# The last two value products of the attention moved among the products of the output projection, and the turning of x's maxima put into the transposing mode

## The chip, the cores and the metric

The kernel runs on one core of a Trainium2 chip. The metric is the time of one execution on the device in microseconds (us), the median over several runs. A profile is one more execution, taken with the hardware profiler, with a trace of every instruction on the five engines: TensorE (PE for its matmuls, PEld for its weight loads), VectorE (DVE), ScalarE (ACT), GpSimd (POOL) and SyncE (SP), which here only issues DMAs.

## The reference, cut to what matters

One encoder layer over 1024 tokens of width 1024, all in float32:

```
h = x @ w_in                                   # 1024 x 1024 by 1024 x 3328
q_a, k_a, v_a, z_a, q_b, k_b, v_b, z_b = split(h)
y_a = neighborhood_attention(q_a, k_a, v_a, rel_pos_bias)     # 8 heads of 64, window 8 x 16 on a grid of 16 x 64
y_b = windowed_gqa_with_sink(rotary(q_b), rotary(k_b), v_b)   # 8 query heads, 2 key heads, |i - j| <= 128
mixed = concatenate([y_a * silu(z_a), y_b * silu(z_b)])
y = mixed @ w_out                              # 1024 x 1024 by 1024 x 1024
out = layer_norm(2 ** 0.25 * x + y, gain, bias)
```

## The kernel before, in words

**Numbers in two halves.** Each operand of a large product is scaled by a power of two and split into a float16 high part and a float16 rest. A product is then three matmuls: high by high, high by rest, rest by high. The scales come from maxima. For x, `x_max` gathers maxima of each partition, line 639 reduces them to `gm` (128 partitions by 1), `x_turn` (L514) brings the 128 values into every partition by a matmul of `gm`, broadcast, with the identity, and `x_scale` (L518) reduces these with VectorE and makes `xsc`, the factor for x's float16 parts. `x_turn` writes to spare columns (320 to 448) of a PSUM bank whose first 320 columns hold a running product of x with the value weights (L627, float32r). Two other places turn maxima the same way, but with `nc.tensor.transpose`: L719 for v and L1086 for w_out.

**The order of the work** around x_turn is written out by hand. From there on TensorE's program is made of "fill" work, which is the projections (L404) and later the output projection (L1165), and of attention work that is put between it. A loop over steps `i` (L1328) runs 128 attention units, four to a quad. In it, per unit: scores (`stage_mm`, L933), bias, sum and minimum on VectorE (L958), exponential on ScalarE (L974), split into two float16 parts on ScalarE (L992) and VectorE (L993), and a DMA that transposes the parts (L999, issued by SP, tile `tr`). Per quad: the value product (`stage_pv`, L1035), 24 matmuls that take the transposed probabilities `tr` and the gathered values `va` and write one half of the bank `ps_t`; and `stage_z` (L1046), where VectorE multiplies that half with the gate into tile `z`. The tables `PV_AT` and `Z_AT` (L1321 to L1324) say at which step each quad's value product and gate multiplication are issued; quads 30 and 31 are the last. `LO` (L1153) is the number of steps that the loop runs past the last unit.

**The fill** is dealt out by `pump_to(u)` (L1056): `FILL_AT` holds steps, `FILL_N` the number of matmuls between one such step and the next, and at each call as many matmuls are issued as the tables say are due. What the tables do not cover follows behind the loop, by `pump(10 ** 6)`. The last fill items are the output projection's first parts, for the four row groups of `mixed` that are done early (tiles m4 to m7, `EO[:4]`): two banks `ps_pj` and one `ps_s` for token tiles 0 to 2, then 24 matmuls into two banks `ps_s` for token tiles 3 and 4, then 12 each into two more banks `ps_s` for the second column half of token tiles 0 and 1. Each matmul is 128x128 by 128x512.

**The end**, `final()` (L1182): the tiles m0 to m3 (the groups that the last value products complete) are split by ScalarE (L1076) and VectorE (L1077); w_out's parts wo8 to wo15 are split by ScalarE (L1121, L1123), VectorE (L1129, L1131) and GpSimd (L1191, L1129); TensorE first multiplies token tile 2's second half for m4 to m7 into `ps_t`, the bank that the value products used, then m0 to m3 for the eight open banks, 24 matmuls for each of the four, and then the remaining token tiles. VectorE adds the residual (L1215) as soon as a bank is complete; the row normalisation and the stores follow. Within `final()` a scheduler of the compiler may change the order; inside the loop the order is that of the code.

Of the kernel before, what the change touches and what calls it, by code (L numbers as in the profile page):

```python
# [38 lines left out]
SCALE_AT = ((4, 6), (7, 2))  # L39
K_ORDER = (5, 0, 6, 1, 7, 2, 3, 4)  # L40
FILL = ORDER[NPRO:]
FILL_AT = [0, 6.6, 13.4, 21.4, 29.4, 37.4, 45.4, 53.4, 61.4, 70, 78.8, 87.6, 96.4, 105, 113, 122, 125, 127, 128.5, 131.5, 136]
ZTAG = {"z3": "zv", "zb3": "zc", "z2": "zs", "zb1": "zd", "zb2": "ze"}
X2POOL = (1, 3, 5)
WVPOOL = (3, 5)
# [29 lines left out]
def hybrid_block(ctx, tc, xT, x, wt, wv, wo, bias, sink, gain, lbias, cos, sin, bmask, out):  # L75
# [305 lines left out]
    def project(name):  # L381
        n = ORDER.index(name)
        w_split(2 * n + 2)
        for half in range(2):
            ps = new_group()
            for k in range(KT):
                if k % 4 == 0:
                    need(w_ops[2 * n + k // 4])
                h, l = parts[2 * n + k // 4]
                if n + 2 < NPRO and half == 0 and k == 4:  # L390
                    w_scan(2 * n + 4)
                if n + 2 < NPRO and half == 1 and k == 0:
                    w_scan(2 * n + 5)
                if half == 0 and k == 4:
                    w_split(2 * n + 3)
                if n + 2 < NPRO and half == 1 and k == 3:
                    z_tree(n + 2)
                if n + 2 < NPRO and half == 1 and k == 7:
                    w_scale(n + 2)
                for i, (a, b) in enumerate(((h, x16h), (h, x16l), (l, x16h))):  # L400
                    mv = b[half, k]
                    if name[0] == "q" and name[1] != "b":
                        mv = mv.rearrange("p (r b c) -> p b r c", b=4, r=8)
                    nc.tensor.matmul(ps, a[:, k % 4, :], mv,  # L404
                                     start=(k == 0 and i == 0), stop=(k == KT - 1 and i == 2))
                    if not (k == KT - 1 and i == 2):
                        yield
            groups.append(evac(name, half, ps))
            yield
# [26 lines left out]
    with ExitStack() as vctx:  # L436
# [76 lines left out]

        def x_turn(ps):  # L514
            nc.tensor.matmul(ps[:, 320:448], gm.to_broadcast([128, 128]), identf, start=False, stop=True,
                             skip_group_check=True)

        def x_scale(ps):  # L518
            nc.vector.tensor_reduce(gm, ps[:, 320:448], axis=AXX, op=ALU.max)
# [97 lines left out]
        for k in range(KT):  # L617
            if k + 3 < KT:
                ahead(k + 3)
            if k + 4 == KT:  # L620
                for j in range(KT):
                    nc.sync.dma_start(x1[j], xT[1, j])
                x_max(6, xh[6].bitcast(F32))
            for ps in FIRST if k == 0 else SECOND if k == 1 else ([(t, a, i) for i in range(3)] for t, a in T1):
                for t, a, i in ps:
                    lh, rh = ((xh, wvh), (xl, wvh), (xh, wvl))[i]
                    nc.tensor.matmul(banks[t, a][:, :320], lh[k][:, 128 * t:128 * t + 128],  # L627
                                     rh[k][:, 320 * a:320 * a + 320],
                                     start=(k == 0 and i == 0), stop=(k == KT - 1 and i == 2))
                if k > 1:  # L630
                    g = T1.index((t, a))
                    if (k, g) == SCALE_AT[0]:
                        wv_scale(banks[t, a])
                        for j in range(KT):
                            wv_hi(j)
                        x_max(7, xh[7].bitcast(F32))
                        for j in range(4):
                            x_max(8 + j, x1pair[j])
                        nc.vector.tensor_reduce(gm, xm, axis=AXX, op=ALU.max)
                        wv_lo(0)  # L640
                    if (k, g) == SCALE_AT[1]:
                        x_turn(banks[t, a])
                        x_scale(banks[t, a])
                        nc.vector.tensor_scalar(vo, vo, xrs, 0.5, op0=ALU.mult, op1=ALU.mult)
# [405 lines left out]
        at(WIN_AT[b], window, b)  # L1050
    run_to(48 * NPRO)
    fill.extend(project(n) for n in FILL)
    FILL_N = [48] * len(FILL) + [9, 9, 6, 12, 24]
    pumped = [0]

    def pump_to(u):  # L1056
        n = 0
        k = int(u) % 4
        u = int(u) // 4 * 4 + 4 * (WARP[k] + (WARP[k + 1] - WARP[k]) * (u - int(u)))
        for k, c in enumerate(FILL_N):  # L1060
            u0, u1 = FILL_AT[k], FILL_AT[k + 1]
            n += int(c * min(max((u - u0) / (u1 - u0), 0), 1))
# [87 lines left out]
            m_ops[e].append(enq("pool", lambda h=h: nc.gpsimd.tensor_sub(  # L1150
                ml[e][:, h], zt[e][:, h], mh[e][:, h]), o))

    LO = 10  # L1153
    NU = len(units)
    def out_mms(t, a, ps, es, c=None):
        o, w = (0, 512) if c is None else LAST[c]
# [162 lines left out]
        stage_mm(us)  # L1319

    PV_AT = {4 * q + 11: q for q in range(30)}  # L1321
    PV_AT.update({131: 30, 135: 31})
    Z_AT = {4 * q + 13: q for q in range(30) if q not in (24, 25, 28, 29)}
    Z_AT.update({115: 24, 116: 25, 128: 28, 129: 29, 132: 30, 136: 31})  # L1324

    clock["step"] = 0
    scan_ops = []
    for i in range(-LD, NU + LO):  # L1328
        if 0 <= i + LD < NU:
# [162 lines left out]
```

## Time and profile before

| | us |
|---|---|
| runs | 441.48, 439.92, 439.67 |
| median of the runs | 439.92 |
| the profiled execution, its own time | 441.73 |
| its span, first to last instruction | 439.9 |
| PE busy | 431.2 |
| DVE busy | 347.8 |
| ACT busy | 298.8 |
| POOL busy | 212.7 |

All times of instructions below are from the profiled execution and count from its span's start. In a timeline row the first number is the start, the second the length from the first start to the last end of the merged instructions, `xN` their number, and what stands in brackets is the idle time of the engine ahead of them and what ended it. The recorded lengths of matmuls overlap, since they are pipelined; the time that one costs is the distance from its start to the next start.

### The profile page before, as it was taken

What the parts mean: (1) busy time and instruction counts of PE and PEld (TensorE: products, weight loads), DVE (VectorE), ACT (ScalarE), POOL (GpSimd) and SP (SyncE); (2) the same over time, 40 slices, a digit from 0 to 9 for tenths busy, and PEclk for the clock granted to TensorE, in tenths of its full rate; (3) what the DMA queues carried; (4) which work ended last, traced back from release to release, by engine and by line L of the source; (5) the groups of instructions that cost most, each with busy time, mean ns of one, the idle gap of its engine ahead of it and who ended that gap; (6) DMA issues with size and microseconds to landing.
All of it is one profiled execution on the core that took longest, in us unless ns stands there. A gap on an engine that the chain in (4) does not pass through costs nothing. (4 is left out here: it accounts for less than half of the span.)

```text
span 439.9 us, 8798 instructions
## 1 busy us (share of the span) xinstructions
PE 431.2 (98%) x2955; PEld 233.2 (53%) x2955; DVE 347.8 (79%) x897; ACT 298.8 (68%) x697; POOL 212.7 (48%) x204
## 2 busy tenths in 40 slices
PE   9999999999999999999999999999999989999994
PEld 8987754444444545454545455554545544444442
DVE  5999947929989988988888887887879739089954
ACT  6798359877577988877889899879787756002211
POOL 0305743564845868356333455566652158005840
PEclk9999999999999999999999999999999999999999
DMA  8992088967946978776999899999999979101721
GB/s 296 343 339 71 5 259 250 302 247 254 322 113 136 168 147 171 141 145 143 173 154 201 138 190 223 192 202 217 216 208 225 193 166 363 41 1 72 262 74 72
DMA packets 133981, 81.72 MB, mean 186 GB/s; under 512 B 101296, under 2 KB 113328, under 8 KB 133680
## 3 DMA queue, kind: packets, MB, share of 16 engines
q1 hardware_dynamic: 133504, 80.67, 74.4%
q8 instruction: 23, 0.38, 0.3%
q10 hardware_dynamic: 432, 0.49, 0.3%
q14 instruction: 22, 0.18, 0.1%
HBM read 50.73 MB, written 9.96 MB: 138 GB/s over the span
## 5 line engine op out<-in xcount | busy, mean ns | idle before, releaser
L404 PE MATMUL ps_pj<-xf,wh 128*128 128x512 f16 x672 | 201.2, 379 | 0.0
L404 PE MATMUL ps_pj<-xf,wl 128*128 128x512 f16 x336 | 127.5, 380 | 0.0
L404 PEld LDWEIGHTS <-wh 128*128 128x128 f16 x672 | 64.9, 98 | 75.4 <-issue 0.8
L1165 PEld LDWEIGHTS <-m 128*128 128x128 f16 x408 | 38.7, 98 | 43.7
L974 ACT ACTIVATE ps_s<-sn,nm 128x385 f32<-128x385 f32 (+3 forms) x96 | 52.1, 543 | 13.9 <-DVE nm L958 12.5
L992 ACT ACTIVATE split<-ps_s,ri 128x384 f16<-128x384 f32 (+2 forms) x96 | 48.5, 539 | 18.3 <-ACT ps_s L974 11.7
L993 DVE SCALAR_TENSOR_TENSOR split<-ps_s,ri,split 128x384 f16<-128x384 f32 (+2 forms) x96 | 52.0, 570 | 5.6 <-ACT split L992 4.6
L1165 PE MATMUL ps_s<-wo,m 128*128 128x512 f16 (+1 forms) x240 | 53.3, 374 | 0.0
L404 PEld LDWEIGHTS <-wl 128*128 128x128 f16 x336 | 32.8, 98 | 38.5 <-issue 0.3
L219 POOL TENSOR_SCALAR wr<-wr,wsc 128x512 f32<-128x512 f32 x26 | 22.4, 862 | 46.9 <-ACT wh L214 45.5
L958 DVE CUSTOM_DVE_ANT_0 sn<-ps_s,bm,nsk 128x384 f32<-128x384 f32 (+1 forms) x64 | 39.7, 635 | 6.6 <-PE ps_s L933 6.4
L901 POOL TENSOR_SCALAR bias<-bias,rsg 128x552 f32<-128x552 f32 (+1 forms) x24 | 20.0, 834 | 45.8 <-DMA bias<-in_bias 33.9
L958 DVE CUSTOM_DVE_ANT_0 sn<-ps_s,bias,sg 128x264 f32<-128x264 f32 (+1 forms) x64 | 33.9, 543 | 2.3 <-PE ps_s L933 1.6
L933 PE MATMUL ps_s<-ks,qs 64*128 64x384 f16 (+4 forms) x384 | 33.4, 305 | 0.1
L220 POOL TENSOR_TENSOR wl<-wr,wh 128x512 f16<-128x512 f32 x26 | 31.8, 1223 | 2.2
L1222 ACT ACTIVATE sd<-mv,eps 128x1 f32<-128x1 f32 x8 | 2.4, 295 | 41.8 <-DVE mv L1220 39.5
L1264 POOL TENSOR_TENSOR xr<-xr,gb 128x512 f32<-128x512 f32 x7 | 11.2, 1607 | 35.9 <-ACT xr L1261 35.9
L993 DVE SCALAR_TENSOR_TENSOR split<-px,ri,split 128x384 f16<-128x384 f32 (+2 forms) x32 | 26.0, 812 | 2.5 <-ACT split L992 2.4
L933 PEld LDWEIGHTS <-qs 64*128 64x128 f16 x384 | 16.2, 94 | 19.5 <-issue 13.3
L681 PEld LDWEIGHTS <-xf 128*128 128x128 f16 x216 | 21.0, 98 | 8.5 <-DVE xf L535 0.3
L1165 PE MATMUL ps_pj<-wo,m 128*128 128x512 f16 (+1 forms) x120 | 24.2, 347 | 0.0
L681 PE MATMUL ps_s<-wf,xf 128*128 128x320 f16 x144 | 23.8, 299 | 0.0
(213 smaller groups left out, 791.0 us busy)
## 6 DMA issues: line engine op xcount, KB each, us to landing
ws<-in_wt SPq DMA_DIRECT2D x15, 512.0 KB, 5.2
wr<-in_wt SPq DMA_DIRECT2D x26, 256.0 KB, 2.9
bias<-in_bias SPq DMA_DIRECT2D x16, 276.0 KB, 3.3
wor<-in_wo SPq DMA_DIRECT2D x16, 256.0 KB, 3.6
xr<-in_x SPq DMA_DIRECT2D x8, 512.0 KB, 7.2
xraw<-in_xT SPq DMA_DIRECT2D x15, 256.0 KB, 5.0
out<-xr SPq DMA_DIRECT2D x14, 256.0 KB, 2.0
bias<-in_bias SPq DMA_DIRECT2D x8, 368.0 KB, 3.8
```

The source lines that it names most:

```text
L219: nc.gpsimd.tensor_scalar(raw, raw, scale, 1.0, op0=ALU.mult, op1=ALU.mult)
L220: nc.gpsimd.tensor_sub(l, raw, h)
L404: nc.tensor.matmul(ps, a[:, k % 4, :], mv, start=(k == 0 and i == 0), stop=(k == KT - 1 and i == 2))
L681: nc.tensor.matmul(ps[:, :320], lh[t // 4, k][:, 128 * (t % 4):128 * (t % 4) + 128], rh[k][:, 320 * a:320 * a + 320], start=(k == first an ...
L901: op = enq("pool", lambda: nc.gpsimd.tensor_scalar(bv, bv, rsg, -1.0, op0=ALU.mult, op1=ALU.mult), ld, prio=0)
L933: nc.tensor.matmul(st[u, "ps"][:, :m], *parts[i], start=i == 0, stop=i == 2)
L958: nc.vector.tensor_tensor_reduce(sn[:, :m], ps[:, :m], bias_t, sg[:, c:c + 1], init, op0=ALU.add, op1=ALU.min, accum_out=nm)
L974: nc.scalar.activation(pt[:, :m], sn[:, :m], AF.Exp, bias=nm, scale=-1.0, accum_out=sm)
L992: nc.scalar.activation(hl[:, :m, 0, :c], src, AF.Copy, scale=ri)
L993: nc.vector.scalar_tensor_tensor(hl[:, :m, 1, :c], src, ri, hl[:, :m, 0, :c], op0=ALU.mult, op1=ALU.subtract)
L1165: nc.tensor.matmul(ps, lh[:, ts], rh[:, cs], start=(e == EO[0] and i == 0), stop=(e == EO[-1] and i == 2))
L1264: nc.gpsimd.tensor_mul(xr[:, h1], xr[:, h1], gb[:, h1])
```

## The change

Six lines change. `x_turn`'s matmul gets `is_transpose=True`. The two last value products move from steps 131 and 135 to 133 and 138, their gate multiplications from 132 and 136 to 135 and 139. The loop runs 13 instead of 10 steps past the last unit, and the 24 matmuls for token tiles 0 and 1, second half, which were issued behind the loop, are dealt out between steps 136 and 140.5.

```diff
-FILL_AT = [..., 122, 125, 127, 128.5, 131.5, 136]
+FILL_AT = [..., 122, 125, 127, 128.5, 131.5, 136, 140.5]
...
             nc.tensor.matmul(ps[:, 320:448], gm.to_broadcast([128, 128]), identf, start=False, stop=True,
-                             skip_group_check=True)
+                             is_transpose=True, skip_group_check=True)
...
-    FILL_N = [48] * len(FILL) + [9, 9, 6, 12, 24]
+    FILL_N = [48] * len(FILL) + [9, 9, 6, 12, 24, 24]
...
-    LO = 10
+    LO = 13
...
-    PV_AT.update({131: 30, 135: 31})
+    PV_AT.update({133: 30, 138: 31})
...
-    Z_AT.update({115: 24, 116: 25, 128: 28, 129: 29, 132: 30, 136: 31})
+    Z_AT.update({115: 24, 116: 25, 128: 28, 129: 29, 135: 30, 139: 31})
```

On ACT, POOL and SP the order of the instructions is the same in both kernels, and on DVE too but for the numbers of PSUM banks. On PE it differs from the first bank for token tiles 3 and 4 on.

TensorE's program before, at the head of quad 30's value product (its values are `va3_2`, its probabilities `tr_4977` and `tr_4981`):

```order
L1165 MATMUL ps_s_5134<-wo2_4493,m7_4027 128x512
L1165 LDWEIGHTS m4_3343
L1165 MATMUL ps_s_5164<-wo0_4316,m4_3343 128x512
L1035 LDWEIGHTS va3_2_4851
L1035 MATMUL ps_t_1842<-tr_4977,va3_2_4851 64x256
```

And the same place now (5167 and 5168 are the banks of token tiles 3 and 4, which were 5164 and 5165):

```order
L1165 LDWEIGHTS m5_3562
L1165 MATMUL ps_s_5168<-wo0_4316,m5_3562 128x512
L1165 LDWEIGHTS m6_3795
L1165 MATMUL ps_s_5167<-wo2_4493,m6_3795 128x512
L1035 LDWEIGHTS va3_2_4851
L1035 MATMUL ps_t_1842<-tr_4977,va3_2_4851 64x256
```

Before, one of the 24 matmuls for token tiles 3 and 4 stood ahead of quad 30's value product; now 13 do, so that it comes 12 matmuls of the output projection later.

TensorE's program before, at the tail of quad 31's value product (`va3_3`, `tr_5076`):

```order
L1035 MATMUL ps_t_1842<-tr_5076,va3_3_4958 64x128
L1165 LDWEIGHTS m7_4027
L1165 MATMUL ps_s_5165<-wo2_4493,m7_4027 128x512
L1165 LDWEIGHTS m4_3343
L1165 MATMUL ps_s_5245<-wo4_5131,m4_3343 128x512
```

And the same place now (5233 is the bank of token tile 1's second half, which was 5258):

```order
L1035 MATMUL ps_t_1842<-tr_5076,va3_3_4958 64x128
L1165 LDWEIGHTS m5_3562
L1165 MATMUL ps_s_5233<-wo4_5131,m5_3562 128x512
L1165 LDWEIGHTS m5_3562
L1165 MATMUL ps_s_5233<-wo4_5131,m5_3562 128x512
L1165 LDWEIGHTS m6_3795
L1165 MATMUL ps_s_5233<-wo6_5153,m6_3795 128x512
```

Between the two value products stood 22 matmuls of the output projection and now stand 27; from quad 31's value product to the first matmul into the bank `ps_t` for token tile 2 there were 25 and now are 8. The sum, 12 + 27 + 8 against 22 + 25, is 47 in both.

VectorE's program from quad 31's gate multiplication on, the same in both kernels:

```order
L1046 SCALAR_TENSOR_TENSOR z3_4879<-ps_t_1842,zcol_113,z3_4879 128x16x16 x2
L1131 SCALAR_TENSOR_TENSOR wo4_5131<-wor5_2619,wos_116,wo4_5131 128x512
L1046 SCALAR_TENSOR_TENSOR z3_4879<-ps_t_1842,zcol_113,z3_4879 128x16x16 x2
L1186 MEMSET eps_5277 128x1
L1077 TENSOR_TENSOR m0_5279<-z0_1052,m0_5279 128x512
L1129 TENSOR_TENSOR wo8_5291<-wor8_2897,wo8_5291 128x512
L1077 TENSOR_TENSOR m1_5280<-z1_1505,m1_5280 128x512
L1129 TENSOR_TENSOR wo11_5302<-wor11_2467,wo11_5302 128x512
L1077 TENSOR_TENSOR m2_5281<-z2_4638,m2_5281 128x512
L1131 SCALAR_TENSOR_TENSOR wo14_5315<-wor14_5145,wos_116,wo14_5315 128x512
```

The third row holds quads 30 and 31; nine operations on the parts of m and wo stand behind it until m0's second half is split (after those shown come m3, wo15 and m0), and none has moved past it.

In `final()` the scheduler also takes m0's matmuls in another order. Before, each of the eight banks got its three in a row. Now seven banks get their high by high matmul first (7 matmuls), then the other two of each bank follow, and token tile 4's bank, which needs m0's second half, gets its three as the 33rd, 34th and 38th matmul from there instead of the 22nd to 24th. From the 49th on the order is as before.

More of the change, by code (lines that the diff above doesn't have):

```diff
@@ L41 @@
 FILL = ORDER[NPRO:]
-FILL_AT = [0, 6.6, 13.4, 21.4, 29.4, 37.4, 45.4, 53.4, 61.4, 70, 78.8, 87.6, 96.4, 105, 113, 122, 125, 127, 128.5, 131.5, 136]
+FILL_AT = [0, 6.6, 13.4, 21.4, 29.4, 37.4, 45.4, 53.4, 61.4, 70, 78.8, 87.6, 96.4, 105, 113, 122, 125, 127, 128.5, 131.5, 136, 140.5]
 ZTAG = {"z3": "zv", "zb3": "zc", "z2": "zs", "zb1": "zd", "zb2": "ze"}
```

## The prediction

> **What bounds the kernel now.** I read the page's busy times first, then what TensorE waited for, then its timeline around the edited place, and last the engines that stand behind that place. The page's first part and the list of TensorE's waits:
>
> ```profile
> PE 431.2 (98%) x2955; PEld 233.2 (53%) x2955; DVE 347.8 (79%) x897; ACT 298.8 (68%) x697; POOL 212.7 (48%) x204
> ...
> PE ps_t L1247 <- ACT dg L1246: 1.5, 1, 1.5
> PE ps_t L1035 <- DMA tr<-split: 1.5, 1, 1.5
> PE ps_t L443 <- PEq L1481: 0.8, 1, 0.8
> ```
>
> TensorE is busy for 431.2 of 439.9 us and waits three times only: at the start, in the last row's normalisation, and once in the middle, for a transposing DMA ahead of a value product. So the time follows TensorE, and a change can win only what TensorE loses: one middle wait of 1.5 us and, perhaps, the turning of x's maxima. Everything moved counts only if TensorE comes to wait for it. TensorE around that wait:
>
> ```profile
> 350.36 2.97 PE L1165 MATMUL ps_s<-wo,m 128*128 128x512 f16 x13
> 354.82 1.18 PE L1035 MATMUL ps_t<-tr,va 128*64 128x256 f16 x24 [1.49 <-DMA tr<-split]
> 355.93 4.92 PE L1165 MATMUL ps_s<-wo,m 128*128 128x512 f16 x22
> 360.78 1.18 PE L1035 MATMUL ps_t<-tr,va 96*64 96x256 f16 x24
> 361.89 5.57 PE L1165 MATMUL ps_s<-wo,m 128*128 128x512 f16 x25
> 367.30 2.75 PE L1165 MATMUL ps_t<-wo,m 128*128 128x512 f16 x12
> 369.89 0.81 PE L1165 MATMUL ps_pj<-wo,m 128*128 128x512 f16 x3
> ```
>
> The second row is quad 30's value product, the fourth quad 31's. The 25 matmuls from 361.89 to 367.30 give 0.216 us each. Quad 31's product starts 0.07 before the recorded end of the matmul ahead of it (355.93 + 4.92 = 360.85 against 360.78), as matmul records overlap; by the same measure quad 30's would have started at 353.33 - 0.07 = 353.26. It started at 354.82, so **the wait costs 1.56 us**, a little over the 1.49 that the row gives.
>
> **The change, part 1: the value products.** Nothing is added or removed; 47 matmuls of the output projection stand in another order around two value products. Twelve move ahead of quad 30's, so TensorE comes to it at 353.26 + 12 x 0.216 = 355.85. Is it ready by then? SP's transposes and their landing:
>
> ```profile
> 351.04 1.22 SPq L999 DMA_TRANSPOSE tr<-split  x1
> ...
> 351.04 3.65 DMA tr<-split
> ...
> 357.07 1.24 SPq L999 DMA_TRANSPOSE tr<-split  x1
> ...
> DMA to landing us min/median/max: 2.7/3.3/4.6
> ```
>
> The transpose that quad 30 waited for was issued at 351.04 and landed 3.65 us later, at 354.69. SP's order is unchanged, and nothing ahead of that transpose waits for a moved matmul, so it lands then in the new kernel too. TensorE is 355.85 - 354.82 = 1.03 us later than the start that the old kernel managed: **the wait goes whole**.
>
> What is late next is quad 31's value product. Its last transpose was issued at 357.07, and the old product began at 360.78 without a wait, so it had landed. The new one: quad 30's product takes 355.93 - 354.82 = 1.11, then 27 matmuls, 5.83, and 0.10 at the switch (355.93 to 360.78 is 4.85 for 22, against 4.75). That is 355.85 + 1.11 + 5.93 = 362.89, 2.1 us later than before and so with at least that much in hand. Had the wait merely vanished with quad 31's place kept, TensorE would have been there at 359.2, ahead of 360.78; that the second product is moved too is what makes the first gain whole.
>
> Now what those moves ask of others. The matmuls pulled ahead need their operands and banks sooner:
>
> ```profile
> 352.34 0.51 DVE L993 SCALAR_TENSOR_TENSOR split<-ps_s,ri,split 128x288 f16<-128x288 f32 x1
> 357.97 1.16 POOL L1134 TENSOR_TENSOR wo<-wor,wo 128x512 f16<-128x512 f32 x1
> ```
>
> Token tile 4's bank is first written three matmuls after token tile 3's, which began as the last of the 13 at 352.95: at 353.60. The last attention unit's split, the last reader of any scores bank, ends at 352.85. The bank for token tile 0's second half follows quad 30's product and eleven matmuls, at 355.85 + 1.11 + 2.38 = 359.34 instead of 362.11; its eleventh matmul, at 361.50, needs w_out's last early rest, which GpSimd ends at 359.13, 2.4 us ahead.
>
> Quad 31's product ends later by 2.1 us, and VectorE sits behind it. Its chain in the old kernel, with the first residual at the end:
>
> ```profile
> 362.01 0.48 DVE L1046 SCALAR_TENSOR_TENSOR z<-ps_t,zcol,z 128x256 f32<-128x256 f32 x1 [5.49 <-PE ps_t L1035]
> 362.42 0.69 DVE L1077 TENSOR_TENSOR m<-z,m 128x512 f16<-128x512 f32 x1
> ...
> 363.02 0.69 DVE L1129 TENSOR_TENSOR wo<-wor,wo 128x512 f16<-128x512 f32 x1
> 363.62 1.10 DVE L1077 TENSOR_TENSOR m<-z,m 128x512 f16<-128x512 f32 x1
> ...
> 367.82 1.64 DVE L1077 TENSOR_TENSOR m<-z,m 128x512 f16<-128x512 f32 x1
> 369.39 1.65 DVE L1131 SCALAR_TENSOR_TENSOR wo<-wor,wos,wo 128x512 f16<-128x512 f32 x1
> 370.96 3.45 DVE L1077 TENSOR_TENSOR m<-z,m 128x512 f16<-128x512 f32 x4
> 386.28 0.75 DVE L1215 SCALAR_TENSOR_TENSOR xr<-ps_pj,oinv,xr 128x512 f32<-128x512 f32 x1 [11.87 <-PE ps_pj L1165]
> ```
>
> The gate multiplication began 1.23 us after its product (362.01 - 360.78), so now at 364.12, and ends at 364.60. Three on TensorE need what is in or behind it. First the bank `ps_t`, which token tile 2 takes over: TensorE is there at 362.89 + 1.11 + 8 x 0.216 = 365.73, **1.1 us after** the multiplication; in the old kernel that was 4.8 us. Second m0 and wo8: TensorE begins m0 at 365.73 + 12 x 0.216 = 368.32, 1.57 before the old 369.89, and its eighth matmul, at 369.83, needs VectorE's first two splits; by the rows these end 1.70 after the multiplication's start (363.71 - 362.01), so at 365.8, 4.0 us ahead. Third m0's second half, the ninth split, ended at 371.82 (370.96 + 0.86); moved by the full 2.1 it ends at 373.9, and its matmul, the 38th, stands at 368.32 + 37 x 0.216 = 376.3, 2.4 us ahead. The old order would have wanted it 14 matmuls sooner, at 373.3: the scheduler's shuffle is what keeps this free. The residuals start when a bank is complete and VectorE had idled 11.87 us ahead of them.
>
> Of DMAs, six loads of x wait for the end of quad 31's product:
>
> ```profile
> 362.00 2.92 SPq L1205 DMA_DIRECT2D xr<-in_x  x6
> ...
> DMA to landing us min/median/max: 5.5/8.5/10.4
> ```
>
> They go out 2.1 us later; the last issue then ends at 367.0, and with the longest landing, 10.4, all are there by 377.4, before the first residual at about 386.28 - 1.56 = 384.7. Part 1: **-1.56 us**.
>
> **Part 2: the turning of x's maxima.** The old trace shows the plain form, and its neighbours on VectorE; and the transposing form at L719:
>
> ```profile
> 28.15 0.49 PE L515 MATMUL ps_s<-identf,gm 128*128 128x128 f32 x2
> 28.40 0.54 PE L627 MATMUL ps_s<-wvh,x 128*128 128x320 f32 x2
> ...
> 28.02 0.88 DVE L512 SCALAR_TENSOR_TENSOR wf<-wvraw,wvs,wf 128x640 f16<-128x640 f32 x1
> 28.81 0.28 DVE L519 TENSOR_REDUCE gm<-ps_s 128x1 f32<-128x128 f32 x1
> ...
> 30.43 1.61 PEld L681 LDWEIGHTS <-xf 128*128 128x128 f16 x13 [0.30 <-DVE xf L535]
> ...
> L719 PE MATMUL ps_s<-identf,vg x1: 272/272/272, 63.5 to 63.5; 128*128 128x128 f32 x1
> ```
>
> The plain form runs as two passes, 0.49 us; the transposing one is one pass of 0.272, so the turn ends 0.22 us sooner, at 28.42 instead of 28.64. Who is waiting? VectorE reads the turned maxima in the reduction at 28.81, 0.17 us after the turn; up to 28.90 it is busy with a split of the value weights (28.02 + 0.88, and its next operation starts 0.09 before a record ends: 362.42 + 0.69 against 363.02). So VectorE, not the turn, sets 28.81. TensorE gains those 0.22 us and gives them back at 30.43, where it waits for the first float16 part of x, made by VectorE behind that reduction. The bounds are 0 and the turn's whole 0.49; a loss is excluded unless the transposing form takes over 0.17 us longer than two passes. I take **0**, as the wait at 30.43 is already there.
>
> **The sum.** 441.73 for the profiled execution's own time, less 1.56, is 440.17. The runs' median, 439.92, lies 1.81 below that execution, close to its span of 439.9; on the median the sum is 439.92 - 1.56 = 438.36, which I give as **438.4**, a gain of 0.35%.
>
> **The rivals.**
>
> *The turn's gain reaches the end.* If VectorE's split of the value weights ends sooner or the reduction waits for the turn after all, 0.22 us come on top: 438.1. Against it speaks that VectorE does not idle ahead of 28.81. The Trainium skill, TensorE: Matmul & The Clock Gate, Terms, has the transposing mode as four times faster for float32; three quarters of 0.49 would be 0.37 and the sum 438.0 by that page's figure, an estimate; the two rows here make it less than twice. Chance 0.09.
>
> *A value product still waits.* The transposes of quads 30 and 31 land later than in the profiled execution. They start to cost once quad 30's lands 1.03 us later; the landings range from 2.7 to 4.6, and quad 30's 3.65 could become 4.6, still inside. Half the wait kept would give 439.1, all of it 439.9. Chance 0.08.
>
> *VectorE's splits come late: slower.* The nine splits behind quad 31's gate multiplication start 2.1 us later, beside GpSimd's own splits:
>
> ```profile
> 365.77 6.29 POOL L1129 TENSOR_TENSOR wo<-wor,wo 128x512 f16<-128x512 f32 x4
> ```
>
> The same kind of operation took 0.69 us at 362.42 and 1.64 at 367.82, beside this row. They must finish by 376.3 and start at 364.12 + 0.41 = 364.53: over 1.31 us each, TensorE waits at its 38th matmul; at the pace of the slow ones, 1.57 (367.82 to 369.39), they end at 378.7, a wait of 2.4 us and 440.8, slower than before by 0.2%. Against it: GpSimd's row ends at 372.06, and only splits beside it are slow; two at 0.60 bring the chain to 365.73, four at 1.57 to 372.01, three more at 0.65 to 373.96. The Trainium skill, Perfetto Trace Analysis, Optimizing Scalar/DVE Operations, says that GpSimd and VectorE share a read port of SBUF; the longer splits beside GpSimd agree with that, and by the rule the later start puts more of the chain beside GpSimd, which speaks against this change. Chance 0.06.
>
> That the change does not do what it says is excluded for part 1, since the built order shows the 12 and 27 matmuls; for part 2 the first rival covers it.
>
> **How the numbers follow.** The forecast has 0.77. The low end is the whole turn won, 438.36 - 0.49, and the 0.25 by which the fastest old run lies under the median: 437.6. The high end takes in half of the wait kept, 439.1, and the same 0.25: 439.4. About 0.5% is what a measurement of this kernel can tell from no change, so the lines are at 437.7 and 442.1. Faster by more needs the first rival and a fast median: 0.08. Slower by more needs the third at nearly twice its price: 0.05. The rest, 0.87, lies between.
>
> **What the changed profile would show.** In TensorE's list of waits the one for `tr<-split` is gone and no new one of over 0.3 us is there; quad 30's value product starts near 355.9, quad 31's near 362.9, token tile 2's first matmul into `ps_t` near 365.7, m0's first near 368.3, and the span ends about 1.6 sooner, near 438.3. At the start, L515 is one matmul of about 0.27 us, the reduction still starts at 28.81 and L681 at 30.43, with a longer idle time ahead. I would be wrong if TensorE waited for VectorE at `ps_t` (1.1 us in hand, the thinnest of all), or at m0's second half, or if transposes kept it at either value product.

## The result, and the profile after

| | before | after |
|---|---|---|
| median of 20 runs each, us | 441.39 (439.67 to 442.58) | 440.31 (439.03 to 442.0) |
| ratio, 95% interval | | 0.9971 (0.9957 to 0.9985) |
| profiled execution, us; its span | 441.73; 439.9 | 440.36; 438.6 |
| granted clock in the profiled execution | 0.998 | 0.997 |

The medians differ by 1.08 us. By the ratio the changed kernel is faster by 0.29%, 1.28 us, with an interval from 0.66 to 1.90. The forecast change, 438.36/439.92 = 0.9965, lies inside that interval, and the whole interval is a change of less than 0.5%, as forecast. The forecast time does not fit: 440.31 lies above the range's end of 439.4. The 20 runs of before include the three shown ahead of the prediction; two of those, 439.67 and 439.92, are the lowest two of the 20, and the other 17 run from 440.88 to 442.58.

The busy times on the page of the changed kernel, to be read against the same line of before:

```profile
PE 431.3 (98%) x2954; PEld 233.4 (53%) x2954; DVE 348.2 (79%) x897; ACT 298.9 (68%) x697; POOL 210.5 (48%) x204
```

TensorE is as busy as before (431.3 against 431.2) in a span 1.3 us shorter. The list of what TensorE waited for in the changed kernel (in total, times, longest) says where these 1.3 us were:

```profile
PE ps_t L1247 <- ACT dg L1246: 1.5, 1, 1.5
PE ps_t L443 <- PEq L1481: 0.8, 1, 0.8
PE ps_t L681 <- DVE xf L535: 0.2, 1, 0.2
```

The wait at L1035, ahead of the value product, is gone. New in the list is the 0.2 us at L681, the first float16 product, where the prediction had TensorE give back what it gains at the turn: the weight load there waited 0.30 us for VectorE before (the row at 30.43 in the prediction) and waits 0.46 now. TensorE's timeline around the moved products in the changed kernel (start, length, engine, line, what):

```profile
348.80 1.18 PE L1035 MATMUL ps_t<-tr,va 128*64 128x256 f16 x24
...
350.57 5.56 PE L1165 MATMUL ps_s<-wo,m 128*128 128x512 f16 x25
356.06 1.18 PE L1035 MATMUL ps_t<-tr,va 128*64 128x256 f16 x24
357.18 6.00 PE L1165 MATMUL ps_s<-wo,m 128*128 128x512 f16 x27
363.11 1.18 PE L1035 MATMUL ps_t<-tr,va 96*64 96x256 f16 x24
364.22 1.90 PE L1165 MATMUL ps_s<-wo,m 128*128 128x512 f16 x8
365.96 2.75 PE L1165 MATMUL ps_t<-wo,m 128*128 128x512 f16 x12
368.55 0.59 PE L1165 MATMUL ps_pj<-wo,m 128*128 128x512 f16 x2
```

Quads 30 and 31, the bank `ps_t` and m0 begin at 356.06, 363.11, 365.96 and 368.55; the prediction had 355.85, 362.89, 365.73 and 368.32. Each is 0.21 to 0.23 late, and so was TensorE when it came there: quad 29's product, the first row, began at 348.80, and in the kernel before at 348.59:

```profile
348.59 1.18 PE L1035 MATMUL ps_t<-tr,va 128*64 128x256 f16 x24
...
432.11 0.86 PE L1241 MATMUL ps_t<-bb,identf 128*128 128x384 f32 x2
```

From there on the two timelines differ by the wait alone; where the 0.21 us ahead of it come from stays open. The second row, the start of the last normalisation, has its counterpart in the changed kernel 1.34 us earlier, which is 1.56 - 0.21:

```profile
430.77 0.86 PE L1241 MATMUL ps_t<-bb,identf 128*128 128x384 f32 x2
```

VectorE behind quad 31, and GpSimd's splits beside it, in the changed kernel:

```profile
364.33 0.49 DVE L1046 SCALAR_TENSOR_TENSOR z<-ps_t,zcol,z 128x256 f32<-128x256 f32 x1 [6.56 <-PE ps_t L1035]
364.74 0.69 DVE L1077 TENSOR_TENSOR m<-z,m 128x512 f16<-128x512 f32 x1
365.35 1.65 DVE L1129 TENSOR_TENSOR wo<-wor,wo 128x512 f16<-128x512 f32 x1
...
370.05 1.64 DVE L1077 TENSOR_TENSOR m<-z,m 128x512 f16<-128x512 f32 x1
371.62 0.74 DVE L1131 SCALAR_TENSOR_TENSOR wo<-wor,wos,wo 128x512 f16<-128x512 f32 x1
...
373.55 2.49 DVE L1077 TENSOR_TENSOR m<-z,m 128x512 f16<-128x512 f32 x4
```

```profile
364.83 6.32 POOL L1129 TENSOR_TENSOR wo<-wor,wo 128x512 f16<-128x512 f32 x4
```

Four splits, from 365.35 to 371.62, ran at 1.57 us each beside GpSimd's row, and the next three at 0.64. The ninth ends at 373.55 + 2.49/4, about 374.2; its matmul stands at 368.55 + 37 x 0.216 = 376.5. At the start of the changed kernel, the turn of x's maxima (L515), its reader (L519) and the first float16 product (L681):

```profile
28.05 0.88 DVE L512 SCALAR_TENSOR_TENSOR wf<-wvraw,wvs,wf 128x640 f16<-128x640 f32 x1
28.85 0.28 DVE L519 TENSOR_REDUCE gm<-ps_s 128x1 f32<-128x128 f32 x1
```

```profile
28.19 0.32 PE L515 MATMUL ps_s<-identf,gm 128*128 128x128 f32 x1
...
30.47 0.31 PE L681 MATMUL ps_t<-wf,xf 128*128 128x320 f16 x1 [0.20 <-DVE xf L535]
```

One pass instead of two; the reader starts when VectorE's split is through, as before, and L681 starts 30.47 - 30.43 = 0.04 us later than before. From line 639's reduction to L681 it is 2.50 us in both.

### The profile page after: what moved, and what is told of

Its sections match the earlier page's. It is cut to its first block, busy times and chain, and to the rows that moved or that the text cites. A ratio compares the mean times of both kernels' runs of the same rounds, so it can differ in the third digit from the quotient of the medians.

```text
span 438.6 us, 8796 instructions
## 1 busy us (share of the span) xinstructions
PE 431.3 (98%) x2954; PEld 233.4 (53%) x2954; DVE 348.2 (79%) x897; ACT 298.9 (68%) x697; POOL 210.5 (48%) x204
## 5 line engine op out<-in xcount | busy, mean ns | idle before, releaser
L933 PE MATMUL ps_s<-ks,qs 64*128 64x384 f16 (+4 forms) x384 | 33.5, 305 | 0.1
L220 POOL TENSOR_TENSOR wl<-wr,wh 128x512 f16<-128x512 f32 x26 | 31.8, 1223 | 2.2
L933 PEld LDWEIGHTS <-qs 64*128 64x128 f16 x384 | 16.2, 94 | 19.6 <-issue 13.3
L681 PEld LDWEIGHTS <-xf 128*128 128x128 f16 x216 | 21.0, 98 | 8.6 <-DVE xf L535 0.5
L681 PE MATMUL ps_s<-wf,xf 128*128 128x320 f16 x144 | 23.8, 299 | 0.0
```

The lines of the kernel that those rows point to most:

```text
L220: nc.gpsimd.tensor_sub(l, raw, h)
L681: nc.tensor.matmul(ps[:, :320], lh[t // 4, k][:, 128 * (t % 4):128 * (t % 4) + 128], rh[k][:, 320 * a:320 * a + 320], start=(k == first an ...
L933: nc.tensor.matmul(st[u, "ps"][:, :m], *parts[i], start=i == 0, stop=i == 2)
```

## The experiments

The main theory is the prediction's: the whole gain is the wait at quad 30, both products have to move for it, and the turn is worth nothing. The rivals are its own: the turn reaches the end, a value product still waits, VectorE comes late.

**The value products alone** (the change without the new mode):

```diff
-                             is_transpose=True, skip_group_check=True)
+                             skip_group_check=True)
```

> Part 1 alone: the two value products moved, the turn of x's maxima as before. Main theory (the whole gain is the one TensorE wait of 1.56 us ahead of quad 30's value product): no wait for the transposing DMA in the list of TensorE's waits, 1.56 us less than before, ratio 0.9965. Rival (a part of the gain is the turn's): 1.3 us less or fewer, and the changed kernel faster than this one by 0.2 us. On the level: if single executions scatter by about 1 us either way at the same clock and the three runs shown of before were low draws, the median of before lies near 441.3 here too; if the later runs were slowed as a session, it lies near 439.9 with little scatter.

Measured: 439.73 us (12 runs) against 441.15 of before (35 runs), ratio 0.9973 (0.9958 to 0.9988), where the whole change had 0.9971. All of the measured gain is there without the new mode. In this execution VectorE, though, did wait for the plain turn:

```profile
27.09 0.88 DVE L512 SCALAR_TENSOR_TENSOR wf<-wvraw,wvs,wf 128x640 f16<-128x640 f32 x1
28.66 0.29 DVE L519 TENSOR_REDUCE gm<-ps_s 128x1 f32<-128x128 f32 x1 [0.70 <-PE ps_s L515]
```

The split of the value weights was done by 27.97 here, against 28.90 in the kernel before, and the reduction idled 0.70 us for the turn. The condition of the first rival, that the reduction waits for the turn, does occur.

**The turn alone** (the kernel before with the new mode):

```diff
-                             skip_group_check=True)
+                             is_transpose=True, skip_group_check=True)
```

> Part 2 alone: the turn of x's maxima in the transposing mode, the value products as before. Main theory: 0.0 us; L515 is one matmul of about 0.3 us, VectorE's reduction L519 still starts as its split of the value weights ends, L681 starts as long after line 639's reduction as before (2.50 us), and TensorE idles longer ahead of it; the wait of 1.5 us for the transposing DMA stays. Rival (the turn is on the path): L681 starts 0.22 us sooner, 0.22 us less.

Measured: 440.81 us, ratio 1.0001 (0.9984 to 1.0018). No gain to be seen, as the main theory has it, though the rival's 0.22 us, a ratio of 0.9995, lies inside the interval too. The trace decides between them: L681 starts 2.51 us behind line 639's reduction (2.50 in the kernel before), with a longer idle time of TensorE ahead of it, 0.20 us. One thing there was not as expected, quad 30's value product in the old place:

```profile
352.98 1.18 PE L1035 MATMUL ps_t<-tr,va 128*64 128x256 f16 x24 [0.40 <-DVE z L1046]
```

The wait is 0.40 us where the kernel before had 1.49, and a gate multiplication of VectorE ends it, not a DMA.

**The first product alone**, quad 30 put later and quad 31 left:

```diff
-    PV_AT.update({131: 30, 135: 31})
+    PV_AT.update({133: 30, 135: 31})
...
-    Z_AT.update({115: 24, 116: 25, 128: 28, 129: 29, 132: 30, 136: 31})
+    Z_AT.update({115: 24, 116: 25, 128: 28, 129: 29, 134: 30, 136: 31})
```

> Before with quad 30's value product alone moved behind 12 more matmuls; quad 31's stays, so that 10 instead of 22 matmuls stand between the two. Main theory: the wait ahead of quad 30 goes, and TensorE comes to quad 31 at 359.2, ahead of its last transpose, which lands at about 360.7: a wait of 1.2 to 1.6 us there, and a time within 0.4 us of before's. Rival (quad 31's transposes land well ahead): no wait, 1.56 us less.

Measured: 440.6 us, ratio 0.9986 (0.9966 to 1.0007). Quad 30 starts without a wait and quad 31 has it instead:

```profile
355.26 1.18 PE L1035 MATMUL ps_t<-tr,va 128*64 128x256 f16 x24
...
359.80 1.18 PE L1035 MATMUL ps_t<-tr,va 96*64 96x256 f16 x24 [1.10 <-DMA tr<-split]
```

In this trace, moving the first product only hands the wait on, a little smaller than the 1.2 to 1.6 us expected. The time can't say it: its interval holds no change at all as well as the 0.9971 of the whole change.

**The second product later still**, right ahead of token tile 2's bank (against the changed kernel):

```diff
-    LO = 13
+    LO = 14
...
-    PV_AT.update({133: 30, 138: 31})
+    PV_AT.update({133: 30, 140: 31})
```

with quad 31's entry in Z_AT at 141 instead of 139.

> The changed kernel with quad 31's value product 8 matmuls later still, so that the bank it writes is taken over by token tile 2 straight behind it. Main theory (the thinnest margin of the change is there, 1.1 us, and 8 matmuls are 1.73): TensorE waits about 0.65 us for the gate multiplication ahead of its first matmul into the bank, and the time is 0.65 us over the changed kernel's, 0.9 under before's. Rival (VectorE's splits behind the gate multiplication come late too): a further wait at m0 and over 2 us more than the changed kernel, slower than before.

Measured: 440.76 us, ratio 1.0 (0.9984 to 1.0015); the products alone, on the same chip, had 0.9973. TensorE's rows:

```profile
363.99 1.18 PE L1035 MATMUL ps_t<-tr,va 96*64 96x256 f16 x24
365.75 2.75 PE L1165 MATMUL ps_t<-wo,m 128*128 128x512 f16 x12 [0.58 <-DVE eps L1186]
```

The row names the small operation that stands just behind quad 31's gate multiplication on VectorE; the multiplication had to read `ps_t` first, and it ended at 365.69, 0.06 us ahead of this row. The margin that the prediction called the thinnest, 1.1 us, is used up when the 8 matmuls, 1.73 us, are gone, and TensorE waits 0.58 us where 0.65 was expected. No further wait came at m0's second half. The time was expected 0.9 us under before's and is not: against the products alone it is 1.03 us more. The two intervals are wide enough to hold a difference of 0.58; what the rest is, if it is real, stays open.

**The kernel before, profiled again.** The 0.40 of the second experiment asked how large the wait is from one execution to the next: four more profiles of the unchanged kernel.

> The kernel before, unchanged, for one more trace. Theory (the wait ahead of quad 30's value product differs from execution to execution, because the transposes' issue on SP and the attention's chain drift by some tenths of a us against TensorE): the wait is between 0.3 and 1.6 us and not the same in the four looks, 1.1 to 1.3 us on average, as much as the timed gain. Rival (it is 1.5 us in every execution, and the changed kernel loses 0.3 us somewhere else): 1.4 to 1.6 us in all four.

> As for the first look: by the theory a wait between 0.3 and 1.6 us that differs from the other looks, by the rival 1.4 to 1.6 us.

> As for the first look: by the theory a wait between 0.3 and 1.6 us that differs from the other looks, by the rival 1.4 to 1.6 us.

> As for the first look: by the theory a wait between 0.3 and 1.6 us that differs from the other looks, by the rival 1.4 to 1.6 us. In all four, where the span is longer than 439.9 us, the excess lies ahead of the first float16 product (L681) or in the batch of scores near 294.6 us, and not behind 372 us.

Measured: 440.52, 440.62, 440.83 and 439.81 us; a run beside them had 441.66. Quad 30 in the first, with VectorE's rows ahead of it:

```profile
346.07 0.52 DVE L958 CUSTOM_DVE_ANT_0 sn<-ps_s,bias,sg 128x288 f32<-128x288 f32 x1 [1.29 <-POOL bias L901]
...
352.28 0.52 DVE L993 SCALAR_TENSOR_TENSOR split<-ps_s,ri,split 128x288 f16<-128x288 f32 x1
352.71 0.87 DVE L1046 SCALAR_TENSOR_TENSOR z<-ps_t,zcol,z 128x256 f32<-128x256 f32 x2
```

```profile
353.63 1.18 PE L1035 MATMUL ps_t<-tr,va 128*64 128x256 f16 x24 [1.12 <-DVE z L1046]
```

and in the second, third and fourth:

```profile
353.71 1.18 PE L1035 MATMUL ps_t<-tr,va 128*64 128x256 f16 x24 [1.02 <-DVE z L1046]
```

```profile
353.90 1.18 PE L1035 MATMUL ps_t<-tr,va 128*64 128x256 f16 x24 [0.73 <-DVE z L1046]
```

```profile
352.93 1.18 PE L1035 MATMUL ps_t<-tr,va 128*64 128x256 f16 x24 [0.77 <-DVE z L1046]
```

The old place waited in all six profiles that have it: 1.49, 1.12, 1.02, 0.73, 0.77 and 0.40 us, 0.92 on average and, with the 0.07 by which records overlap, 1.0 lost. So the wait differs from execution to execution, as the theory had it, but its average is under the 1.1 to 1.3 us that the theory gave. All four spans are under 439.9 us (438.0 to 439.0), so what the fourth expectation says of longer spans was not tested. In five of the six the product starts 0.04 to 0.05 after the end of the gate multiplications of quads 28 and 29 (352.71 + 0.87 = 353.58 against 353.63), which read the two halves of `ps_t`. By the code quad 30 writes only the half that the first of the two reads, and that one ended at 353.19; the product starts behind the second all the same. They stand on VectorE's queue behind the last attention units, which in this execution waited 1.29 us for a bias that GpSimd makes. In the profiled execution of before the second multiplication ended at 353.63 as well, but the transpose landed another 1.06 later, at 354.69. It was issued late: SP took 12.15 us there to issue eight transposes,

```profile
346.16 12.15 SPq L999 DMA_TRANSPOSE tr<-split  x8
```

and in the first of the four profiles 11.54:

```profile
345.88 11.54 SPq L999 DMA_TRANSPOSE tr<-split  x8
```

The fourth of the eight is the last that quad 30 needs. Taken singly, the third took 2.11 us to issue in the one and 1.28 in the other, so that the fourth was issued at 351.04 against 350.04, and it landed after 3.65 us against 3.1. Why the third took longer stays open.

**The changed kernel, profiled again**, unedited:

> The changed kernel, unchanged, beside the three variants below. Theory (the gain is the wait ahead of quad 30's value product, which was 0.4 to 1.5 us in six traces of the old tail, mean 0.9): ratio to before 0.997 to 0.998, no wait at either value product, and the median again near 440 and above 439.4. Rival (the first comparison was high): a ratio of 0.9965 and a median near 438.4.

Measured: 440.5 us (438.6 to 443.15) against 441.73 of before (35 runs), ratio 0.9971 (0.9947 to 0.9995): the same gain a second time. Its trace has one wait for the transposes after all, one quad earlier:

```profile
348.96 1.18 PE L1035 MATMUL ps_t<-tr,va 128*64 128x256 f16 x24 [0.94 <-DMA tr<-split]
```

This is quad 29's product, which the change doesn't move. Quads 30 and 31 did not wait, here or in any trace with both moved. For quad 30 it was close: the fourth transpose was issued at 352.35 and landed 3.7 us later, at about 356.1, and the product began at 356.23. Its old place lay 353.26 - 348.59 = 4.67 us behind quad 29's start, here at 353.63, so by these rows the old order would have waited about 2.6 us in this execution, an estimate.

**The split that hides the turn, put later**, once with the plain turn and once with the new mode, both on the changed kernel. The split of the first value weights moves behind the splits of x:

```diff
-                        wv_lo(0)
...
-        for k in range(1, KT):
+        for k in range(KT):
             wv_lo(k)
```

> The changed kernel with the turn in its old, plain form, and VectorE's split of the value weights' first block moved behind the first float16 parts of x, so that nothing stands on VectorE between the reduction to the 128 maxima and the reduction of the turned ones. Theory: the turn is now waited for: L519 starts within 0.1 us of the plain turn's end, 0.6 to 0.7 us after the turn starts, instead of 0.65 to 0.9; L681 starts 0.1 to 0.2 us sooner after L515 than in the changed kernel (2.28). Rival (the wait moves to a later split of the value weights): TensorE waits for VectorE between 30 and 40 us.

> As e5, with the turn in the transposing mode. Theory: with the split out of the way the mode is worth its 0.2 us: L519 starts 0.4 to 0.45 us after L515, and L681 about 0.2 us sooner after L515 than in e5. By the time, 0.2 us are under what the comparison can tell. Rival (the mode is worth nothing even then): the two distances as in e5.

Measured: 440.76 us, ratio 0.998 (0.996 to 1.0), with the plain turn; 440.57 us, 0.997 (0.9951 to 0.9988), with the new mode. With nothing in front of it the reader waits for the turn in both. The plain turn and its reader:

```profile
28.44 0.38 PE L515 MATMUL ps_s<-identf,gm 128*128 128x128 f32 x2
...
30.49 0.31 PE L680 MATMUL ps_t<-wf,xf 128*128 128x320 f16 x1
```

```profile
28.86 0.29 DVE L519 TENSOR_REDUCE gm<-ps_s 128x1 f32<-128x128 f32 x1 [1.20 <-PE ps_s L515]
```

and the new mode:

```profile
28.45 0.27 PE L515 MATMUL ps_s<-identf,gm 128*128 128x128 f32 x1
...
30.39 0.31 PE L680 MATMUL ps_t<-wf,xf 128*128 128x320 f16 x1
```

```profile
28.76 0.29 DVE L519 TENSOR_REDUCE gm<-ps_s 128x1 f32<-128x128 f32 x1 [1.40 <-PE ps_s L515]
```

From turn to reader it is 0.42 us plain and 0.31 in the new mode; L680, which is L681 before the line is taken out, comes 2.05 and 1.94 us behind the turn. So the mode is worth 0.11 us where the turn is on the path, half of the 0.22 of the first rival and of the second expectation. The reader also followed the plain turn sooner, by 0.42 us, than the 0.6 to 0.7 expected. Putting the split later brings nothing beyond that: both traces have a new wait of TensorE for VectorE, near 50 us and so later than the rival of the first expectation put it,

```profile
PE ps_t L261 <- DVE zc L264: 0.7, 1, 0.7
```

in the same words, and neither ratio can be told from the 0.9971 of the unedited change beside them.

**VectorE's scale steps one attention step later** (on the changed kernel). Along the way TensorE's rows showed a batch of scores that takes 0.88 us in some traces and longer in others, with no wait in the list. In the kernel before and the changed kernel:

```profile
294.57 1.34 PE L933 MATMUL ps_s<-ks,qs 64*128 64x264 f16 x12
```

```profile
294.61 1.42 PE L933 MATMUL ps_s<-ks,qs 64*128 64x264 f16 x12
```

The edit takes three small steps of VectorE out of the place where it is late for that batch:

```diff
-        if WO_MAX + 4 <= i < WO_MAX + 7:
-            wo_scale(i - WO_MAX - 4)
+        if WO_MAX + 5 <= i < WO_MAX + 8:
+            wo_scale(i - WO_MAX - 5)
```

> The changed kernel with the three small steps that make w_out's scale on VectorE (L1091 to L1098) one loop step later. In the traces TensorE loses 0 to 0.7 us in the batch of scores near 294.6 us, where VectorE's splits give up the banks late; two of those steps, 0.43 us, stand ahead of these splits. Theory: the batch takes 0.88 us as in the undisturbed traces, and 0.2 to 0.4 us are gained on the changed kernel on average. Rival (the splits are late for GpSimd's sake, whose pieces stretch one of them from 0.64 to 1.4 us): the batch still takes over 1.0 us.

Measured: 440.29 us (439.34 to 440.9), ratio 0.9961 (0.9943 to 0.998). The batch, and the split of VectorE ahead of it:

```profile
294.36 0.88 PE L933 MATMUL ps_s<-ks,qs 64*128 64x264 f16 x12
```

```profile
289.25 1.56 DVE L993 SCALAR_TENSOR_TENSOR split<-px,ri,split 128x384 f16<-128x384 f32 x1
```

The batch is short although the split ran long, as the edit was meant to have it. That alone doesn't show that the edit did it: the second of the four later profiles of the kernel before has a batch of 0.88 behind a split of 1.42 as well. 0.9961 is the lowest ratio of all kernels here, but its interval covers the 0.9971 of the unedited change beside it (440.5 us): inconclusive.

## Why the prediction was right and where it was wrong

**What bounds the kernel, and the wait that goes: right.** TensorE's busy time did not change, the wait left the list, and the end moved by what TensorE no longer lost.

**The wait's size, -1.56 us: this step failed.** "The wait costs 1.56 us" is right for the one execution it was read from, and that one was the largest of six; on average the old place lost 1.0. The timed change can't separate 1.0 from 1.56: it is 1.2 to 1.3 us by the ratios of the change, of its repeat and of the products alone, and each interval holds both (for the change, 0.66 to 1.90). So the size is judged by the traces. The question "is it ready by then?" was put to the transpose alone. The product has a second condition, that VectorE has read `ps_t`, and in five of the six executions that one came last. With 12 matmuls more, 2.6 us, both were met in every trace that has the new order.

The changed kernel's own profile bears on this. There the gate multiplication of quads 28 and 29 is VectorE's

```profile
353.99 0.87 DVE L1046 SCALAR_TENSOR_TENSOR z<-ps_t,zcol,z 128x256 f32<-128x256 f32 x2
```

and ends at 354.86. The old place would have been at 348.80 + (353.26 - 348.59) = 353.47, so that execution would have waited about 1.4 us in the old order. The new one came at 356.06, with 1.2 us in hand. Estimated the same way for all eight traces with quad 30 moved, from quad 29's start, the end of these multiplications and the landing of the fourth transpose, the old order would have waited 0.3 to 1.4 us in seven and 2.6 in the second profile of the changed kernel; with the six that have the old order the average is 1.1.

**The base, 439.92: this step failed by more.** "On the median the sum is 439.92 - 1.56" took three runs as the level. Medians of before are 441.39 (20 runs), 441.15 and 441.73 (35 each, with the experiments), 1.2 to 1.8 higher. The range's end took 0.25 us from those three for the scatter of runs, while single executions of the changed kernel run from 439.03 to 442.0 at granted clocks of 0.995 to 0.999. Single runs as low as 439.67 do occur: three of the 35 beside the first experiment lie between 439.39 and 439.43. So chance in a sample of three is enough to explain it; that these three ran under other conditions isn't excluded. The profiled execution's 441.73, also in hand, was close to the level of the longer series; the prediction saw that it lay 1.81 above the median, and followed the median. The forecast time is 1.9 us low: 1.47 from the base, the other 0.5 from the gain, 1.08 by the medians instead of 1.56. The prediction's first sum, 441.73 - 1.56 = 440.17, came within 0.14 of the result, but by luck: its level was 0.34 too high and its gain 0.48 too large.

**The second product's move: right.** Without it, the wait stands at quad 31 with 1.10 us, in the one trace that has this order; the times alone don't tell.

**The margins behind it: right, but for which is the thinnest.** `ps_t` had room for 1.1 us in the prediction; taking away 8 matmuls, 1.73 us, turned it into a wait of 0.58, so 1.15 was there. The ninth split was to have 2.4 us; it had 2.3. The prediction called the 1.1 at `ps_t` the thinnest margin of all, yet its own 1.03 at quad 30 was thinner, and in the second profile of the changed kernel 0.1 was left of it. The third rival's mechanism took place, four splits at 1.57 beside GpSimd, and stayed inside the margin, as the count against it had said. The same operation took 0.69 us at 364.74 and 1.65 at 365.35, when GpSimd's row was running. The Trainium skill, Perfetto Trace Analysis, Optimizing Scalar/DVE Operations, says that the two share a read port of SBUF; the two lengths agree with that.

**The turn's 0: right, though its reason doesn't hold in every execution.** The split stands ahead of the reduction in twelve of the traces. In ten it covers the turn, and L681 starts 2.50 or 2.51 us behind line 639's reduction, with the plain turn (six) and the new mode (four) alike: nothing is gained. In the values alone the split ended 0.7 us ahead of the reduction, and in the kernel with the later scale steps 0.06. TensorE came to the turn late there, 1.23 and 0.70 us behind line 639's reduction where it is 0.2 to 0.4 otherwise, and from the turn to L681 it took 2.06 us plain and 1.95 in the new mode. So the gain is 0.11 us where the turn is on the path, below what 12 runs can show.

**The second rival: not at the products that were moved.** Late transposes still stopped TensorE at quad 29, by 0.94 and 0.18 us in two of the seven traces with both products moved. At quad 30 one came 0.1 us short of it. What was late there was the issue, at 352.35, and not the landing behind it, 3.7 us; the rival had looked at the landings alone.

## What to carry to other kernels

A wait read from one trace is a sample: before its length becomes a term, ask what else that instruction waits for and how late that was, and take the level and the scatter from many runs rather than from three. When a late operand stops the bounding engine, moving the first consumer can merely hand the wait to the next one, so move each in turn, and count the margin of whatever reads the results. A faster form of an instruction is worth what its reader was really waiting for, and this may be nothing in one execution and a little in the next.

## What the runs showed of the hardware that was not expected

A wait inside a batch of matmuls needs not show in the list of waits. Twelve L933 matmuls were one row of 0.88, 1.34, 1.42 and, in the kernel with the second product later still, 1.58 us,

```profile
293.71 1.58 PE L933 MATMUL ps_s<-ks,qs 64*128 64x264 f16 x12
```

with nothing ahead of them in the list. Taken singly, in the kernel before the eighth began at 295.39, 0.43 us behind the seventh, where the pairs ahead of it follow at 0.11 to 0.15. Of that step 0.15 us is idle, too little for the list, and the rest lies under the seventh's recorded length of 0.28. So a row, and busy time, can hold some waiting. The kernel with the second product later still started this batch 0.86 us earlier than the kernel before (293.71 against 294.57) and ended it 0.62 earlier: part of an early start is given back there. That a release by VectorE is what the batch waits for is argued from the kernel's code, not shown: the experiment on it was inconclusive.

VectorE's split ahead of that batch took from 0.64 to 1.60 us, and its end goes by GpSimd. In the values alone, the split and then GpSimd's row:

```profile
289.31 0.64 DVE L993 SCALAR_TENSOR_TENSOR split<-px,ri,split 128x384 f16<-128x384 f32 x1
```

```profile
289.50 1.47 POOL L1150 TENSOR_TENSOR m<-z,m 128x512 f16<-128x512 f32 x1
```

and in the kernel before:

```profile
290.15 1.32 DVE L993 SCALAR_TENSOR_TENSOR split<-px,ri,split 128x384 f16<-128x384 f32 x1
```

```profile
289.90 1.16 POOL L1150 TENSOR_TENSOR m<-z,m 128x512 f16<-128x512 f32 x1
```

Where VectorE began 0.2 us ahead, its split took 0.64 and GpSimd's operation 1.47; where GpSimd began 0.25 ahead, it took 1.16 and the split 1.32. Over all fourteen traces the split ended 0.41 to 0.42 us after the recorded end of a GpSimd operation that was running when it began, or that began within 0.03 us of it: this one (290.15 + 1.32 = 291.47 against 289.90 + 1.16 = 291.06) in ten, and the one ahead of it (L220) in four, the values alone among them, where that one ended at 289.54. So where in GpSimd's row the split begins changes its time by up to 1 us. The first float16 product began anywhere from 29.67 to 30.47 in the traces with the unedited start. Such shifts, at the same clock, are where the traces of one kernel differ; which of them makes the 3 us between the fastest and the slowest run stays open.
